# A two-layer diffusion trunk in float32 pairs: a reordered prologue, factors that change engine, and a shorter inverse root

## The chip, the cores and the metric

The kernel runs on one core of one Trainium2 chip. The metric is the device time of one launch, in microseconds (us): the median of the runs shown. The core has five instruction queues that run side by side and are tied together by semaphores: PE (matrix product, with PEld for its weight loads), DVE (VectorE), ACT (ScalarE), POOL (GpSimd) and SP, which here issues every DMA. Each queue runs in the order in which it was written.

## The reference

There are 512 latent and 256 context tokens of width 1024, and two layers. Each layer normalises (root mean square), scales and shifts the stream with vectors that come from a conditioning vector c ("adaLN": `c @ w_ada + b_ada`, six vectors of 1024 a layer), and projects the result with one wide matrix `w_in`. Four mixers work on pieces of that projection:

```
a = s5_branch(...)      # diagonal complex state space, both directions, GLU
b = sgu_branch(...)     # u * (W_s @ layer_norm(v) + b), blocks of 128 tokens
c = ssd_branch(...)     # silu(conv3(xbc)), chunked scan, rms_norm(y * silu(z))
d = mla_branch(...)     # q, k = rms_norm(.) * g, rotary part, softmax(q k^T / sqrt(96)) v
out = sum_i sigmoid(gate_i) * (y_i @ w_branch[i]) @ w_out
```

A residual, a second normalisation and a SwiGLU feed-forward follow. The output is the latent stream after layer two; context reads only context.

## The kernel before

Activations are kept transposed: a tile holds 128 channels on its partitions and the tokens along its rows (context 0 to 255, latents 256 to 767). A float32 product is made of three products of rounded halves (`mm3`): each weight tile is cast on ACT (`whi`), the remainder is made on POOL or DVE (`wlo`), and each activation likewise has a high and a low part (`hh`, `hl`; tiles `h`, `g` or `f`). PE accumulates in two PSUM banks `acc` and, for all else, in four banks `b`. A bank is free for the next product only when the last engine that reads it is done.

**Order.** The program is written once, as Python generators that interleave the mixers (`mix`), and a scheduler then fixes each engine's order with its own timing model; the trace shows how that order runs on the chip. In `mix`, the attention units (`attend`, two heads and 256 queries each) are interleaved with the gating unit (`sgu`), the state-space sixths (`s5_prep`, `s5_sixth`) and a filler made of wide projections at low priority: the convolution's input (`conv` in `mix`) and z. All of these share DVE. SP keeps eight loads in flight: the issue of a load waits until the load eight places ahead of it has landed.

**Prologue.** `run` loads the constants and c, then all six row blocks of the stream (`load_x`: context first), ten small parameter rows (`params_load`), eight column chunks of w_ada with 256 columns each (`ada_load`: rows of 1 KB), and the first 256 columns of w_in. `turn_x` transposes the stream on PE, `ada_chunk` multiplies a chunk and puts its result column-wise into `mod`, and `norm_mod` sums squares, takes `rsqrt` on DVE, spreads the result over partitions with a product against `ones`, and makes `hh` and `hl`.

**Places the change touches.** `rsqrt` (eleven short DVE instructions) is called by every normalisation: norm_mod, the attention's q and k, sgu and ssd. `mla_pair` scales each head with its token's factor and the learned gain by one `stt` a head, six a tile; `attend_unit` divides the exponentials by their sums on DVE; `conv`'s callback reads its PSUM bank five times (DVE, DVE, DVE, then ACT writes the tanh back into the bank, then DVE):

```
s.ts(a, ps, w(1), q["cb"][:, c:c + 1], ALU.mult, ALU.add)
... two stt that read ps shifted by a token ...
s.act(ps, a, AF.Tanh)
s.stt(a, ps, 1.0, a, ALU.add, ALU.mult)
```

In `ssd` the carried-in part of a chunk's output enters a PSUM bank as a 128-wide product with the identity, and the chunk's own part is added by products that are 64 wide, two to a bank column.

## Time and profile before

| | before |
|---|---|
| median of 3 runs | 2835.06 us (2834.6 to 2836.26) |
| profiled execution: span from first to last instruction | 2833.9 us (no other time of that execution is listed; 1.2 us below the median) |
| PE busy | 2639.4 us, 93% |
| DVE busy | 1562.5 us, 55%, 3402 instructions |
| ACT busy | 870.4 us, 31%, 1693 instructions |
| POOL busy | 1210.8 us, 43% |
| mean granted TensorE clock | 0.974 |

A busy share is a mean over stages with different limits. Three kinds of view are read below: the sum of a stretch (windows), the order of time (timeline), and the idle time of an engine by what ended it (waits). In waits and timelines the part behind `<-` names the engine and tile that came last.

### The profile page before, as it was taken

How to read it: one execution, taken by the hardware profiler on the slowest of the kernel's cores; microseconds unless marked ns; L12 is line 12 of the kernel's file. 1: busy time of each engine (PE TensorE's matmuls, PEld its weight loads, DVE VectorE, ACT ScalarE, POOL GpSimd, SP SyncE). 2: the span in 40 equal slices, each digit the busy share in tenths (PEclk: the TensorE clock that was granted, in tenths of full speed). 3: DMA queues.
4: the chain of work that ended last, by engine and by line, in shares of the span. 5: the costliest groups of instructions: out<-in, count | busy, mean ns of one | idle time of the engine just before them, and what ended most of it. 6: DMA issues, size and time to landing. Idle time of an engine off the chain costs nothing. (4 is left out here: it accounts for less than half of the span.)

```text
span 2833.9 us, 40144 instructions
## 1 busy us (share of the span) xinstructions
PE 2639.4 (93%) x14950; PEld 2147.7 (76%) x14950; DVE 1562.5 (55%) x3402; ACT 870.4 (31%) x1693; POOL 1210.8 (43%) x901
## 2 busy tenths in 40 slices
PE   6998898999999987999999999899999989899999
PEld 4777676777888875888888877777666866678887
DVE  6678989758453769543221245677836546422111
ACT  4233332342232333222212234333343223322222
POOL 2254444314432836554333334442423537344543
PEclk9999899999999998999999999999999989999999
DMA  7655454454444645323322335556445536323332
GB/s 247 175 176 188 138 168 141 145 162 143 138 155 149 213 139 169 108 91 94 97 76 60 94 98 159 179 175 192 139 152 167 167 127 206 114 84 105 104 97 82
DMA packets 430106, 397.46 MB, mean 140 GB/s; under 512 B 52292, under 2 KB 379640, under 8 KB 429816
## 3 DMA queue, kind: packets, MB, share of 16 engines
q1 hardware_dynamic: 429912, 394.91, 45.4%
q8 instruction: 118, 1.93, 0.3%
q14 instruction: 76, 0.62, 0.1%
HBM read 305.79 MB, written 89.05 MB: 139 GB/s over the span
## 5 line engine op out<-in xcount | busy, mean ns | idle before, releaser
L174 POOL TENSOR_TENSOR wlo<-raw,whi 128x1024 fp32r<-128x1024 f32 (+2 forms) x314 | 632.3, 2015 | 1064.9 <-ACT whi L169 982.9
L193 PE MATMUL acc<-h,whi 128*128 128x512 f32 (+2 forms) x3424 | 1020.8, 368 | 30.6 <-DVE gs L186 22.6
L193 PE MATMUL acc<-h,wlo 128*128 128x512 f32 (+1 forms) x2024 | 745.8, 369 | 7.8 <-DVE wlo L174 5.1
L193 PEld LDWEIGHTS acc<-h,whi 128*128 128x128 f32 (+1 forms) x3424 | 612.0, 191 | 142.4 <-DVE gs L186 25.7
L169 ACT CAST whi<-raw 128x1024 fp32r<-128x1024 f32 (+2 forms) x390 | 324.9, 834 | 817.1 <-PE b L193 304.8
L193 PEld LDWEIGHTS acc<-h,wlo 128*128 128x128 f32 x2024 | 384.5, 190 | 76.4 <-DVE wlo L174 7.1
L193 PE MATMUL acc<-g,whi 128*128 128x512 f32 (+1 forms) x840 | 271.4, 396 | 20.4 <-DVE g L174 8.5
L193 PE MATMUL acc<-f,whi 128*128 128x512 f32 (+1 forms) x600 | 230.2, 393 | 6.3 <-POOL f L174 5.2
L193 PE MATMUL b<-g,whi 128*128 128x256 f32 (+1 forms) x840 | 215.7, 335 | 3.3 <-ACT whi L169 3.3
L193 PE MATMUL b<-h,wlo 128*128 128x256 f32 (+1 forms) x624 | 203.6, 326 | 2.1 <-POOL wlo L174 2.1
L193 PE MATMUL b<-h,whi 128*128 128x256 f32 (+1 forms) x624 | 203.4, 326 | 0.0
L193 PEld LDWEIGHTS acc<-g,whi 128*128 128x128 f32 x840 | 153.9, 193 | 56.4 <-DVE g L174 11.9
L193 PE MATMUL b<-f,whi 128*128 128x256 f32 (+1 forms) x600 | 186.7, 321 | 1.7 <-ACT whi L169 1.7
L193 PE MATMUL b<-g,g 128*64 128x128 f32 (+5 forms) x915 | 180.4, 357 | 8.0 <-ACT g L171 5.2
L193 PEld LDWEIGHTS b<-g,whi 128*128 128x128 f32 x840 | 148.8, 193 | 28.4 <-ACT whi L169 6.5
L193 PE MATMUL acc<-g,wlo 128*128 128x512 f32 (+1 forms) x372 | 148.2, 398 | 4.7 <-DVE wlo L174 4.5
L186 DVE SCALAR_TENSOR_TENSOR sc<-sc,acc 128x512 f32<-128x512 f32 (+1 forms) x45 | 30.6, 680 | 219.6 <-ACT sc L171 219.6
L193 PEld LDWEIGHTS b<-g,g 128*128 128x128 f32 (+2 forms) x915 | 121.1, 182 | 34.2 <-issue 13.5
L174 POOL TENSOR_TENSOR g<-sc,g 128x256 fp32r<-128x256 f32 (+2 forms) x81 | 88.2, 1090 | 126.7 <-ACT g L169 87.9
L193 PEld LDWEIGHTS acc<-f,whi 128*128 128x128 f32 x600 | 112.8, 189 | 31.5 <-POOL f L174 6.7
L174 POOL TENSOR_TENSOR f<-f,f 128x384 f32<-128x384 f32 (+2 forms) x84 | 102.8, 1229 | 78.7 <-DVE f L174 35.0
L174 POOL TENSOR_TENSOR g<-g,sc 128x512 f32<-128x512 f32 (+1 forms) x82 | 103.0, 1268 | 75.8 <-DVE g L186 37.9
(257 smaller groups left out, 4013.2 us busy)
## 6 DMA issues: line engine op xcount, KB each, us to landing
raw<-in_w_in_dram SPq DMA_DIRECT2D x50, 1024.0 KB
raw<-in_w_ffn_in_dram SPq DMA_DIRECT2D x88, 512.0 KB
raw<-in_w_ada_dram SPq DMA_DIRECT2D x41, 1024.0 KB
raw<-in_w_ffn_out_dram SPq DMA_DIRECT2D x36, 512.0 KB
gate<-gs SPq DMA_DIRECT2D x32, 384.0 KB
f<-s5w SPq DMA_DIRECT2D x48, 256.0 KB
raw<-in_w_branch_dram SPq DMA_DIRECT2D x32, 384.0 KB
gs<-gate SPq DMA_DIRECT2D x32, 384.0 KB
```

The costliest lines, as they stand in the source:

```text
L169: s.nc.scalar.copy(out=out, in_=x)
L174: (e or s.nc.vector).tensor_tensor(out=out, in0=a, in1=b, op=op)
L186: s.nc.vector.scalar_tensor_tensor(out=out, in0=a, scalar=sc, in1=b, op0=op0, op1=op1)
L193: s.nc.tensor.matmul(out=out, lhsT=l, rhs=r, start=start, stop=stop)
```

## The change

Six edits. (1) The prologue loads three parameter rows and the four latent blocks, then four w_ada chunks of 512 columns (rows of 2 KB), then the two context blocks, then the other small rows; latents are transposed first, context last. (2) `rsqrt` has nine instructions in place of eleven. (3) In `mla_pair` one product with a broadcast replaces six `stt` a tile; the gain goes into the evacuation of the transposes (a per-partition factor on ACT and DVE) and into rotary tables made once a layer on DVE (`rot`), with four more small loads a layer into `gain`. (4) These scalings move from DVE to ACT: the softmax division, the value rows of `mla_pair`, the first step of `conv`, and sgu's normalisation (with one small DVE instruction more). (5) `conv` writes its tanh to an SBUF tile instead of its PSUM bank. (6) The identity product in `ssd` is made in two halves of 64 columns.

```diff
@@ -200,16 +200,18 @@
-        shape = list(x.shape)
-        hx, t = s.ty(shape), s.ty(shape)
+        t, u = s.ty(list(x.shape)), s.ty(list(x.shape))
         s.ts(y.bitcast(I32), x.bitcast(I32), -0.5, float(0x5F3759DF), ALU.mult, ALU.add)
-        s.ts(hx, x, -0.5)
-        for _ in range(3):
-            s.mul(t, y, y)
-            s.mul(t, t, hx)
-            s.stt(y, t, 1.5, y, ALU.add, ALU.mult)
+        s.mul(t, y, y)
+        s.mul(t, t, x)
+        s.ts(u, t, 0.375, -1.25, ALU.mult, ALU.add)
+        s.mul(u, u, t)
+        s.stt(y, u, 1.875, y, ALU.add, ALU.mult)
+        s.stt(t, y, -0.5, y, ALU.mult, ALU.mult)
+        s.mul(t, t, x)
+        s.stt(y, t, 1.5, y, ALU.add, ALU.mult)
@@ -295,12 +297,13 @@
-        return s.params_rest(l, s.params_load(l))
-    def params_load(s, l):
+        return s.params_rest(l, s.params_load(l)[0])
+    def params_load(s, l, first=10):
...
+        later = []
@@ -311,10 +314,12 @@
-            s.dma.dma_start(out=rows[at:at + n, :], in_=ap)
+            later.append((rows[at:at + n, :], ap))
...
-        return rows, names, at
+        for o, ap in later[:first]:
+            s.dma.dma_start(out=o, in_=ap)
+        return (rows, names, at), lambda: [s.dma.dma_start(out=o, in_=ap) for o, ap in later[first:]]
@@ -336,7 +341,18 @@
-        q["qn"], q["kn"] = bc("qn", t["mla_q_norm"][l], 96), bc("kn", t["mla_k_norm"][l], 96)
+        q["rot"] = {}
+        gain = q["gain"] = s.keep("gain", [96, 4])
+        s.nc.vector.memset(gain, 1.0)
+        for i, (part, ap) in enumerate((("q", t["mla_q_norm"][l]), ("kv", t["mla_k_norm"][l]))):
+            g = bc("gn" + part, ap[64:96], 32).rearrange("p (o a d) -> p o a d", o=1, a=2).to_broadcast([P, 4, 2, 16])
+            gt = q["rot"][part] = s.keep("rot" + part, [P, 2, 4, 2, 16])
+            for j, c in enumerate((K_COS, K_SIN)):
+                cs = s.k[:, c:c + 64].rearrange("p (b o d) -> p b o d", b=4, o=1).to_broadcast([P, 4, 2, 16])
+                s.mul(gt[:, j], g, cs)
+            s.dma.dma_start(out=gain[:, 2 * i:2 * i + 1], in_=ap.rearrange("(d o) -> d o", o=1))
+            s.dma.dma_start(out=gain[:64, 2 * i + 1:2 * i + 2], in_=ap[:64].rearrange("(d o) -> d o", o=1))
@@ -369,47 +385,47 @@
-    def ada_load(s, l, i, tag="raw"):
-        src = s.t["w_ada"][l][:, 256 * i:256 * i + 256].rearrange("(k p) f -> p k f", p=P)
-        out = []
-        pool, step = {"raw": (s.rp, KD), "h": (s.hp, 3), "f": (s.fp, 2)}[tag]
-        for k in range(0, KD, step):
-            n = min(step, KD - k)
-            raw = pool.tile([P, n, 256], F32, tag=tag, name=s.nm(tag))
-            s.dma.dma_start(out=raw, in_=src[:, k:k + n])
-            out += [raw[:, j] for j in range(n)]
+    def ada_load(s, l, i, tags=("raw",), w=256):
+        src = s.t["w_ada"][l][:, 256 * i:256 * i + w].rearrange("(k p) f -> p k f", p=P)
+        out, each = [], KD // len(tags)
+        for h, tag in enumerate(tags):
+            pool, size = {"raw": (s.rp, 2048), "h": (s.hp, 768), "f": (s.fp, 512)}[tag]
+            n = min(each, size // w)
+            for k in range(each * h, each * h + each, n):
+                raw = pool.tile([P, n, w], F32, tag=tag, name=s.nm(tag))
+                s.dma.dma_start(out=raw, in_=src[:, k:k + n])
+                out += [raw[:, j] for j in range(n)]
         return out
-    def ada_chunk(s, a, i, raw=None):
+    def ada_chunk(s, a, i, raw=None, w=256):
         raw = s.ada_load(a["l"], i) if raw is None else raw
-        both = s.acc() if a["l"] == 0 or i >= 8 else s.b1()
-        ps = both[:, :256]
+        nb = w // P
+        ps = (s.acc() if a["l"] == 0 or i >= 8 else s.b1())
+        p2 = (ps[:, 256:] if nb == 2 else s.b1()).rearrange("p (b j v) -> p b j v", b=nb, j=4)
+        ps = ps[:, :w]
...
-        s.act(part[:, :256], ps)
-        p2 = both[:, 256:].rearrange("p (b j v) -> p b j v", b=2, j=4)
-        for b in range(2):
+        s.act(part[:, :w], ps)
+        for b in range(nb):
             s.tr(p2[:, b], part[:, b * P:(b + 1) * P])
-        m = a["m"]
-        s.nc.vector.tensor_reduce(out=m[:, 2 * i:2 * i + 2, :], in_=p2[:, :, :, 0:2].rearrange("p b j v -> p b v j"),
-                                  axis=AX.X, op=ALU.add)
-        s.add(m[:, 2 * i:2 * i + 2, :], m[:, 2 * i:2 * i + 2, :],
-              a["q"]["b_ada"][:, 2 * i:2 * i + 2].unsqueeze(2).to_broadcast([P, 2, 2]))
-        j, c = i // 4, slice(2 * (i % 4), 2 * (i % 4) + 2)
-        m = m[:, 2 * i:2 * i + 2, :]
+        m = a["m"][:, 2 * i:2 * i + nb, :]
+        s.nc.vector.tensor_reduce(out=m, in_=p2[:, :, :, 0:2].rearrange("p b j v -> p b v j"), axis=AX.X, op=ALU.add)
+        s.add(m, m, a["q"]["b_ada"][:, 2 * i:2 * i + nb].unsqueeze(2).to_broadcast([P, nb, 2]))
+        j, c = i // 4, slice(2 * (i % 4), 2 * (i % 4) + nb)
...
-            s.stt(v, m, 1.0, g.unsqueeze(2).to_broadcast([P, 2, 2]), ALU.add, ALU.mult)
+            s.stt(v, m, 1.0, g.unsqueeze(2).to_broadcast([P, nb, 2]), ALU.add, ALU.mult)
@@ -420,18 +436,17 @@
+        raw = s.rp.tile([P, 2, D], F32, tag="raw", name=s.nm("raw"))
         for b in range(NB):
-            if b == 4:
-                raw = s.rp.tile([P, 2, D], F32, tag="raw", name=s.nm("raw"))
-            x = raw[:, b - 4] if b >= 4 else s.wp.tile([P, D], F32, tag="whi" if b % 2 else "wlo", name=s.nm("xr"))
-            src = s.t["ctx"][0, b * P:(b + 1) * P, :] if b < 2 else s.t["x"][0, (b - 2) * P:(b - 1) * P, :]
-            s.dma.dma_start(out=x, in_=src)
-            out.append(x)
-        return out
+            out.append(raw[:, b] if b < 2 else s.wp.tile([P, D], F32, tag="whi" if b % 2 else "wlo", name=s.nm("xr")))
+        src = lambda b: s.t["ctx"][0, b * P:(b + 1) * P, :] if b < 2 else s.t["x"][0, (b - 2) * P:(b - 1) * P, :]
+        for b in range(2, NB):
+            s.dma.dma_start(out=out[b], in_=src(b))
+        return out, lambda: [s.dma.dma_start(out=out[b], in_=src(b)) for b in range(2)]
...
-        for b in range(0, NB, 2):
+        for b in (2, 4, 0):
@@ -550,8 +565,9 @@
+            s.stt(x, mv[:, :, 0], -1.0, r, ALU.mult, ALU.mult)
             for j in range(2):
-                s.ts(vn[:, j, :], vn[:, j, :], mv[:, j, 0:1], r[:, j:j + 1], ALU.subtract, ALU.mult)
+                s.act(vn[:, j, :], vn[:, j, :], AF.Identity, scale=r[:, j:j + 1], bias=x[:, j:j + 1])
@@ -629,7 +645,7 @@
-                    s.ts(vt[:, b, hs, :], pv[:, :, 64:P], r[:, b:b + 1])
+                    s.act(vt[:, b, hs, :], pv[:, :, 64:P], AF.Copy, scale=r[:, b:b + 1])
@@ -646,20 +662,16 @@
-        gn = q["qn"] if part == "q" else q["kn"]
+        gt, gc = q["rot"][part], q["gain"][:, 2 * (part == "kv") + (off == CTX):][:, :1]
...
-            for h in range(6):
-                s.stt(x[:, h, :w], x[:, h, :w], rr[:, b, h:h + 1], gn[:, :w], ALU.mult, ALU.mult)
+            s.mul(x[:, :, :w], x[:, :, :w], rr[:, b, :].unsqueeze(2).to_broadcast([P, 6, w]))
             if part == "kv":
-                kg = s.ty([P, 1, 32])
-                s.mul(kg, kr[:, b:b + 1, :], gn[:, 64:].unsqueeze(1))
-                s.mul(x[:, :, 64:96], kg.to_broadcast([P, 6, 32]), rs[:, b, :].unsqueeze(2).to_broadcast([P, 6, 32]))
+                s.mul(x[:, :, 64:96], kr[:, b:b + 1, :].to_broadcast([P, 6, 32]), rs[:, b, :].unsqueeze(2).to_broadcast([P, 6, 32]))
             if off == CTX:
-                cs, sn = (s.k[:, j + 16 * (b0 + b):j + 16 * (b0 + b) + 16].unsqueeze(1).unsqueeze(1).to_broadcast([P, 6, 2, 16])
-                          for j in (K_COS, K_SIN))
+                cs, sn = (gt[:, i, b0 + b].unsqueeze(1).to_broadcast([P, 6, 2, 16]) for i in range(2))
@@ -670,8 +682,8 @@
-            s.act(y[:, 0:3], ps[0][:96])
-            s.vcopy(y[:, 3:6], ps[1][:96])
+            s.act(y[:, 0:3], ps[0][:96], AF.Copy, scale=gc)
+            s.ts(y[:, 3:6], ps[1][:96], gc)
@@ -724,7 +736,7 @@
-                s.ts(p[b][:, :nk * P], p[b][:, :nk * P], ri[:, b:b + 1])
+                s.act(p[b][:, :nk * P], p[b][:, :nk * P], AF.Copy, scale=ri[:, b:b + 1])
@@ -856,7 +868,8 @@
-                    s.mm(o, yoff[:, 2 * c:2 * c + 2, :].rearrange("p h e -> p (h e)"), s.ident, stop=False)
+                    for h2 in range(2):
+                        s.mm(o[64 * h2:64 * h2 + 64, :], yoff[:, 2 * c + h2, :], s.ident, stop=False)
@@ -1333,11 +1346,12 @@
-                s.ts(a, ps, w(1), q["cb"][:, c:c + 1], ALU.mult, ALU.add)
+                s.act(a, ps, AF.Identity, scale=w(1), bias=q["cb"][:, c:c + 1])
...
-                s.act(ps, a, AF.Tanh)
-                s.stt(a, ps, 1.0, a, ALU.add, ALU.mult)
+                z = s.sc()[:, :n]
+                s.act(z, a, AF.Tanh)
+                s.stt(a, z, 1.0, a, ALU.add, ALU.mult)
@@ -1490,17 +1504,19 @@
-        xr = s.load_x()
-        rows = s.params_load(0)
-        order = (0, 4, 1, 5, 2, 6, 3, 7)
-        aw = [s.ada_load(0, i, tag) for i, tag in zip(order, ["raw"] + 5 * ["h"] + 2 * ["f"])]
+        rows, more = s.params_load(0, 3)
+        xr, x_ctx = s.load_x()
+        order = (0, 4, 2, 6)
+        aw = [s.ada_load(0, i, tags, 512) for i, tags in zip(order, (("h", "h"), ("h", "h"), ("f", "f"), ("f", "raw")))]
+        x_ctx()
+        more()
...
-            s.ada_chunk(a, i, w)
+            s.ada_chunk(a, i, w, 512)
```

Three places of the new order matter for what follows; in the rows a name is tile, number, `<-` and what it reads.

In the prologue SP's queue reaches the first w_in load (`raw_197` before, `raw_207` now) so; before:

```order
L379 DMA f_195<-in_w_ada_dram 128x2x256
L479 DMA raw_197<-in_w_in_dram 128x8x256
L334 DMA alog_313<-in_ssd_a_log_dram 128x12
L334 DMA dtb_315<-in_ssd_dt_bias_dram 128x12
L334 DMA qn_317<-in_mla_q_norm_dram 128x96
```

Now, the last eleven rows of the small loads ahead of it:

```order
L339 DMA gnq_329<-in_mla_q_norm_dram 128x32
L354 DMA gain_327<-in_mla_q_norm_dram 96x1
L355 DMA gain_327<-in_mla_q_norm_dram 64x1
L339 DMA gnkv_336<-in_mla_k_norm_dram 128x32
L354 DMA gain_327<-in_mla_k_norm_dram 96x1
L355 DMA gain_327<-in_mla_k_norm_dram 64x1
L360 DMA bs_343<-in_sgu_b_s_dram 64x3x128
L361 DMA dd_344<-in_ssd_d_dram 64x3x1
L360 DMA bs_343<-in_sgu_b_s_dram 64x3x128
L361 DMA dd_344<-in_ssd_d_dram 64x3x1
L494 DMA raw_207<-in_w_in_dram 128x8x256
```

The load stood directly behind w_ada; now nineteen small loads and the context (which shares its tile's buffer) stand between. On DVE, in the same stretch, the context's copies (`g_213`, `g_215`, ...) now stand behind the rotary tables:

```order
L174 TENSOR_TENSOR sc_452<-sc_452,sc_472 128x512
L174 TENSOR_TENSOR rotq_331<-gnq_329,k 128x128 x2
L174 TENSOR_TENSOR rotkv_338<-gnkv_336,k 128x128
L458 COPY g_213<-b_285 128x256
L174 TENSOR_TENSOR rotkv_338<-gnkv_336,k 128x128
L458 COPY g_215<-b_293 128x256
L458 COPY g_217<-b_301 128x256
L458 COPY g_219<-b_309 128x256
L190 TENSOR_SCALAR hc_321<-prm_319 128x20
L416 TENSOR_REDUCE mod_349<-b_355 128x8
```

So these copies, and what stands behind them, follow the small load `gnkv`.

Second place: POOL ahead of the first projection (h: low part of a normalised tile; wlo: remainder of w_in). Before:

```order
L174 TENSOR_TENSOR h_472<-sc_532,h_464 128x512
L174 TENSOR_TENSOR h_474<-sc_544,h_466 128x512
L174 TENSOR_TENSOR h_475<-sc_550,h_467 128x512
L174 TENSOR_TENSOR h_476<-sc_556,h_468 128x512
L174 TENSOR_TENSOR h_478<-sc_568,h_470 128x512
L174 TENSOR_TENSOR wlo_200<-raw_197,whi_199 128x1024
L174 TENSOR_TENSOR wlo_1101<-raw_197,whi_1100 128x1024
L174 TENSOR_TENSOR h_479<-sc_574,h_471 128x512
```

Now:

```order
L174 TENSOR_TENSOR wlo_210<-raw_207,whi_209 128x1024
L174 TENSOR_TENSOR wlo_1069<-raw_207,whi_1068 128x1024
L174 TENSOR_TENSOR h_444<-sc_502,h_436 128x512
L174 TENSOR_TENSOR h_446<-sc_514,h_438 128x512
L174 TENSOR_TENSOR h_447<-sc_520,h_439 128x512
L174 TENSOR_TENSOR h_448<-sc_526,h_440 128x512
L174 TENSOR_TENSOR h_450<-sc_538,h_442 128x512
L174 TENSOR_TENSOR h_451<-sc_544,h_443 128x512
```

The two remainders moved from behind five of the six low parts to ahead of all six.

Third place: DVE at the first convolution tile of layer one's mixing (`gs` is the result, `acc` its PSUM bank, `ty` and `g` the softmax sums and exponentials). Before:

```order
L190 TENSOR_SCALAR gs_4404<-acc_4405,hc_311 128x512
L174 TENSOR_TENSOR ty_4308<-ty_4308,ty_4312 128x2
L186 SCALAR_TENSOR_TENSOR gs_4404<-acc_4405,hc_311,gs_4404 128x511
L725 RECIPROCAL ty_4309<-ty_4308 128x2
L708 TENSOR_REDUCE ty_4334<-b_4331 128x2
L186 SCALAR_TENSOR_TENSOR gs_4404<-acc_4405,hc_311,gs_4404 128x511
L190 TENSOR_SCALAR g_4321<-g_4321,ty_4309 128x768
L190 TENSOR_SCALAR g_4322<-g_4322,ty_4309 128x768
L714 TENSOR_REDUCE ty_4338<-b_4340 128x1
L714 TENSOR_REDUCE ty_4338<-b_4343 128x1
L186 SCALAR_TENSOR_TENSOR gs_4404<-acc_4405,gs_4404 128x512
```

Now DVE has, and ACT has in its own queue:

```order
L174 TENSOR_TENSOR ty_4207<-ty_4207,ty_4211 128x2
L737 RECIPROCAL ty_4208<-ty_4207 128x2
L174 TENSOR_TENSOR f_5046<-f_5046,f_5047 128x512
L186 SCALAR_TENSOR_TENSOR gs_4275<-acc_4276,hc_321,gs_4275 128x511 x2
L186 SCALAR_TENSOR_TENSOR gs_4275<-sc_4304,gs_4275 128x512
```

```order
L171 ACTIVATE g_4221,ty_4211<-b_4215,ty_4206 128x512
L171 ACTIVATE gs_4275<-acc_4276,hc_321 128x512
L171 ACTIVATE g_4220<-g_4220,ty_4208 128x768
L171 ACTIVATE g_4221<-g_4221,ty_4208 128x768
L171 ACTIVATE sc_4304<-gs_4275 128x512
L169 CAST whi_4618<-raw_4616 128x1024
```

DVE's last read of the bank is now the second `stt`; the first step, the two divisions and the tanh stand in ACT's queue, the weight cast behind them.

## Rows read from the trace of the kernel before

**Rows 1.** The page, head and part 1: span, then busy time by engine.

```profile
span 2833.9 us, 40144 instructions
...
PE 2639.4 (93%) x14950; PEld 2147.7 (76%) x14950; DVE 1562.5 (55%) x3402; ACT 870.4 (31%) x1693; POOL 1210.8 (43%) x901
```

**Rows 2.** Windows of both mixing stages: busy PE, PEld, DVE, ACT, POOL; clock; DMA.

```profile
150.00:700.00 550.00, 490.33 (x3128) 397.21 (x3126) 442.77 (x1062) 193.51 (x464) 223.94 (x201) 0.95 0.50 156
...
1800.00:2320.00 520.00, 488.01 (x2802) 374.17 (x2801) 341.87 (x872) 176.67 (x386) 196.10 (x158) 0.97 0.52 161
```

**Rows 3.** Timeline of SP, 0 to 60 us: start, duration of issue, load.

```profile
14.94 0.40 SPq L379 DMA_DIRECT2D raw<-in_w_ada_dram  x1
...
37.41 0.37 SPq L479 DMA_DIRECT2D raw<-in_w_in_dram  x1
...
40.24 0.44 SPq L334 DMA_DIRECT2D qn<-in_mla_q_norm_dram  x1
...
46.05 0.60 SPq L345 DMA_DIRECT2D dd<-in_ssd_d_dram  x1
```

**Rows 4.** DMA, 0 to 60 us: rate in 40 slices of 1.5 us.

```profile
GB/s 0 217 154 363 401 418 421 370 54 4 40 328 369 350 352 348 347 348 348 352 346 348 348 346 348 350 349 347 331 174 56 0 15 186 389 398 410 422 408 432
```

**Rows 5.** Timeline of the prologue: start, duration, what, [idle before it].

```profile
20.36 1.93 PE L193 MATMUL acc<-raw,cT 128*32 128x256 f32 x16 [3.35 <-DMA raw<-in_w_ada_dram]
...
46.30 1.98 ACT L169 CAST whi<-raw 128x1024 fp32r<-128x1024 f32 x2
...
47.70 5.08 POOL L174 TENSOR_TENSOR wlo<-raw,whi 128x1024 fp32r<-128x1024 f32 x2
...
50.31 0.80 PE L193 MATMUL acc<-h,wlo 128*128 128x512 f32 x1 [0.76 <-POOL wlo L174]
...
62.77 0.59 PE L193 MATMUL b<-sc,ones 128*128 128x256 f32 x2
...
65.59 0.50 PE L193 MATMUL acc<-h,whi 128*128 128x256 f32 x2 [2.22 <-POOL h L174]
```

**Rows 6.** Waits of PE, 150 to 700 us: total us, times, longest.

```profile
PE acc L193 <- DVE gs L186: 14.1, 5, 5.1
PE b L197 <- DVE g L186: 11.7, 1, 11.7
PE b L193 <- DVE sc L443: 9.9, 5, 3.5
```

**Rows 7.** The same, 1700 to 2400 us.

```profile
PE acc L193 <- DVE gs L186: 8.5, 4, 3.5
```

**Rows 8.** Timeline at one convolution tile, 396 to 403 us.

```profile
399.04 0.74 DVE L186 SCALAR_TENSOR_TENSOR gs<-acc,hc,gs 128x511 f32<-128x511 f32 x1
...
401.94 0.68 DVE L186 SCALAR_TENSOR_TENSOR gs<-acc,gs 128x512 f32<-128x512 f32 x1
...
402.68 1.22 PE L193 MATMUL acc<-h,whi 128*128 128x512 f32 x2 [3.41 <-DVE gs L186]
```

**Rows 9.** Groups of DVE by form: count | busy us, mean ns | idle before.

```profile
L190 DVE TENSOR_SCALAR g<-g,ty 128x768 f32<-128x768 f32 x48 | 31.2, 690 | 0.3
...
L186 DVE SCALAR_TENSOR_TENSOR g<-g,ty,kn 128x64 f32<-128x64 f32 x72 | 21.7, 365 | 0.0
...
L174 DVE TENSOR_TENSOR ty<-ty 128x2 f32<-128x2 f32 x68 | 19.6, 289 | 1.4
...
L174 DVE TENSOR_TENSOR sc<-f,ty 128x384 f32<-128x384 f32 x20 | 14.5, 747 | 0.3
```

**Rows 10.** Groups of ACT by form, the same columns.

```profile
L171 ACT ACTIVATE g<-b,ty 128x256 f32<-128x256 f32 x60 | 28.3, 473 | 70.2 <-DVE ty L190 64.3 <-DVE ty L174 3.3 <-DVE ty L186 1.7
...
L169 ACT CAST g<-st 128x768 fp32r<-128x768 f32 x5 | 4.2, 836 | 9.0 <-DMA st<-mq 8.9
```

**Rows 11.** Groups of PE by form: the identity product, and half-width products.

```profile
L193 PE MATMUL b<-g,g 128*64 128x128 f32 x240 | 22.5, 303 | 0.0
...
L193 PE MATMUL b<-k,sc 128*128 128x128 f32 x60 | 14.8, 331 | 1.4 <-POOL sc L174 1.4
```

## Prediction

> **What bounds the kernel now.** I read the page first: PE is busy for 93% of a span of 2833.9 us [rows 1], so a gain is a stretch in which PE stands still or runs slowly. The sums by stretch then show where that is. In the mixing stage of layer one (150 to 700 us) PE is busy 490.3 of 550 us at a clock of 0.95, and DVE 442.8; in that of layer two (1800 to 2320 us) PE is busy 488.0 of 520 us at 0.97, and DVE 341.9 [rows 2]. That is 59.7 + 32.0 = 91.7 us of idle PE beside an engine that is 81% and 66% busy. The waits name it: of the first stage's idle time 14.1 us end with DVE's work on a convolution tile, 11.7 us (one wait) with DVE's scaling of an attention tile, and 9.9 us with DVE's copies of transposed probabilities [rows 6]; in the second the convolution takes 8.5 us [rows 7]. So here the bound is DVE's queue. The third place is the prologue: PE's projection runs steadily only from 50.31 us [rows 5].
>
> **The prologue, +8 us.** Before: one chunk of w_ada (1.05 MB) is issued at 14.94 us [rows 3] onto an empty queue and multiplied at 20.36 us [rows 5]: 5.4 us, of which 3.0 are data at 348 GB/s, so 2.4 are fixed. Rows of 4 KB (the stream, 4.5 to 12 us) move at 363 to 421 GB/s, rows of 1 KB (w_ada) at 346 to 352 [rows 4]. For rows of 2 KB there is no row; between 16 engines at 47 ns a piece (348) and 158 ns (415), a straight line gives 84 ns, 390 GB/s, my estimate; the ends are 348 and 415.
> Now: the latents' 2.1 MB are issued three small loads later (0.44 us each [rows 3]) and flow from about 5 to 10.3 us; w_ada's 8.39 MB take 21.5 us at 390, to 31.8; the context 2.5 us, to 34.3. In the old queue data ended near 44.3 us [rows 4] and the load waiting for it was issued at 46.05 [rows 3]: 1.7 us to completion, so 36.0 now. With eight loads in flight, the first broadcast load waits for that; `gnkv` is five issues behind it (0.46 us each, 38.3) and lands 2.4 us later, 40.7. DVE's queue holds the context's copies behind the tables made from it; two tables, three copies and the last transposes take about 1.9 us: 42.6. Only then is the context's buffer free for w_in, whose issue also stands behind ten more small loads, near 42 us. It lands 5.4 us later, at 48.1; before, it was there by 46.05. ACT casts it (1.98 us for two [rows 5]), POOL makes the two remainders (5.08 us for two [rows 5]) from 49.1 to 54.2, and only behind them the first low part of the activations (half as wide as a remainder, 1.27 us): PE starts at 55.5, not 50.31, +5.2. The 48 products take 12.4 us as before (50.31 to 62.77). The context's sum of squares then stands on PE behind the last of them, where before its spreading product was ready at 62.77, 2.8 us ahead of the context's first product [rows 5]; another inverse root, about 2.6 us, now lies between. Together +8. Bounds: +12 with w_ada at 348; -3 if none of the small loads is waited for and the hole at 12 to 15 us [rows 4] closes.
>
> **The convolution, -17 us.** In the tile shown the second `stt` ends at 399.8 us, but the bank is free only after the last one, at 402.6, because ACT's tanh and two softmax divisions lie between; PE stood for 3.4 us [rows 8]. Now nothing reads the bank after the second `stt`: 2.8 us earlier. The nine waits sum to 14.1 + 8.5 = 22.6 us [rows 6, 7], the longest 5.1; taking 2.8 us from each, or all of the shorter ones, leaves about 5. What may come late next is ACT, which now makes the first step. Bounds -23 and +5.
>
> **The softmax division, -5 us.** 48 divisions of 690 ns [rows 9] leave DVE, two in front of most of the copies that PE waited 9.9 us for [rows 6]: 1.4 us from each of five waits is 7, of which I take 5. On ACT one costs what a cast of the same size costs, 836 ns [rows 10], and ACT is busy only 193.5 and 176.7 us in the stages [rows 2]. Bounds -10, +5.
>
> **The rest of DVE's relief, -8 us.** Off DVE go 31.2 us of divisions, 21.7 us of 64-wide scalings [rows 9], 60 wider ones (at least 365 ns each, 22), some 65 instructions of conv, values, sgu and short divisions (near 0.5 us, estimated, 33), and 44 inverse roots by two instructions of 289 ns [rows 9], 25. On come ten products of 576 and twelve of 384 elements, at 747 ns for 384 [rows 9], 20 us. Net 113 of 785 us in the two stages, 14%. Of the 91.7 us of idle PE, 59 are neither convolution nor copies: 14% is 8. Bounds 0 and -20. A product of two tensors costs 1.95 ns an element and a division 0.90 [rows 9]. The Trainium skill (VectorE: DVE Perf Modes, "Why `tensor_tensor` can't do 2×_2P or 4×") speaks against this exchange: a float32 tensor with a scalar uses both read ports for one tensor and does two elements a cycle, two tensors cannot. With the new products at the division's price, the relief would be 11 us larger, and the sum 1 us lower; the trace agrees with the rule.
>
> **Inverse roots in the norms, -3 us.** Seven norms stand on PE's path, two instructions of 289 ns less each [rows 9], some shorter in a quiet queue: 3. Bounds 0, -6.
>
> **The identity product, -3 us.** Its 60 instructions are busy 14.8 us, 247 ns each; half-width ones 94 ns each [rows 11], so 120 make 11.3. Bounds -4 and, with the old busy time each, +15. The Trainium skill (TensorEngine Tiling (Array Packing), "Key Properties") says that a change of tiling mode drains the engine; here a full-width product stood between half-width ones, so by the rule the gain is more than the rows' 3.5 us. No row prices a drain.
>
> **The clock, -11 us.** At 0.95 of 490.3 us and 0.97 of 488.0 us [rows 2], 24.5 + 14.6 = 39 us of work are lost to the lower of the two levels (1.2 and 2.4 GHz). The three terms above remove 30 of 91.7 us of idle time, a third; I take 11. Bounds 0, -39.
>
> **New waits on ACT, +6 us.** In each of 30 softmax halves ACT's scaling waits for DVE's reciprocal, with evacuations and weight casts behind it. Waits of this kind exist: ACT waited 64.3 us for DVE's maxima [rows 10]. I take 0.2 us of PE a half; bounds 0 and +45 (1.5 us). The parameter loads of layer two and the tables lie beside the feed-forward and cost nothing there.
>
> Sum: 8 - 17 - 5 - 8 - 3 - 3 - 11 + 6 = -33. From the span of 2833.9 that is 2800.9; the median of the runs lies 1.2 us above the span, so 2802 us.
>
> **Rivals.**
> *More relief.* DVE's queue loosens as a whole, half of the 91.7 us goes, and the clock regains 20: -46 - 20 + 8 - 3 + 1 = -60, 2774 us. For it: DVE is named in all four large waits. Against: part of the idle time ends with other data.
> *Little relief.* The new order forms new waits in the same stages: convolution -12, norms -2, halves -3, clock -5, prologue +8, ACT +6: -8, 2827 us. For it: the order comes from a timing model, and each engine is bound to it. With the prologue at its upper bound, +12, this is 2831, no change.
> *Slower: ACT's queue.* Place: the softmax halves, where ACT now waits for DVE, and behind it the evacuations that free PE's banks. At 1.5 us of PE a half, 30 halves give +45 in place of +6, with all else as forecast: 2841 us. It decides from 1.3 us a half on, where 39 us eat up the other terms' 39. For it: 64.3 us of such waits [rows 10]. Against: ACT is 35% busy in these stages [rows 2].
>
> **How the numbers follow.** Forecast (2788 to 2822) 0.45, more relief 0.17, little relief 0.13, no change 0.08, slower 0.17. The range is 2772 to 2842: it holds most of the first four and about half of the slower case. A change within 0.2% (5.7 us) can't be told from none; faster is 0.45 + 0.17 + 0.13 = 0.75, same 0.08, slower 0.17.
>
> **What would show it.** Right: PE's first steady product near 55 us and the context's near 73; waits of PE for `gs` in the mixing stages near 5 us instead of 22.6; DVE's busy time near 1450 us (1562 less 113), ACT's near 935 (870, 40 for the 48 divisions and some 25 for the rest); a clock near 0.98. Wrong: w_in cast before 46 us (prologue); waits of PE for ACT's copies or casts that grow by more than 20 us (ACT's queue); the same idle time behind other names (little relief).

## The result and the profile after

The changed kernel takes 2803.2 us in the median of 4 runs (2799.7 to 2808.2), the kernel before 2834.8 (2829.4 to 2836.3): a ratio of 0.9899, 95% interval 0.9882 to 0.9916, or 28.6 us less (24 to 33); the medians lie 31.6 us apart. The prediction was 2802, 33 us less than before, in a range of 2772 to 2842. The total was right within a few microseconds; several of its terms were not, and they cancelled.

The page of the changed kernel, head and part 1, answers to [rows 1]:

```profile
span 2798.5 us, 39916 instructions
...
PE 2634.6 (94%) x14946; PEld 2139.2 (76%) x14946; DVE 1465.7 (52%) x3084; ACT 942.2 (34%) x1802; POOL 1211.7 (43%) x901
```

PE's work is 4.8 us shorter and its idle time falls from 194.5 to 163.9 us, 30.6 less: the gain is nearly all idle time, where the forecast had 11 of its 33 us as work at a higher clock. The two traced executions lie 35 us apart, some 7 more than the ratio says, so the last digits of what is read from them belong to them alone. DVE lost 97 us (113 forecast), ACT gained 72 (65 forecast). The windows of the two mixing stages, as in [rows 2], and the waits of PE in the first and in the second of them, as in [rows 6, 7]:

```profile
150.00:700.00 550.00, 509.42 (x3242) 408.17 (x3241) 401.19 (x917) 240.36 (x541) 236.81 (x208) 0.96 0.52 162
...
1800.00:2320.00 520.00, 493.46 (x2842) 376.96 (x2841) 318.97 (x735) 213.22 (x440) 214.38 (x173) 0.98 0.56 173
```

```profile
PE b L197 <- DVE g L174: 11.1, 3, 9.1
...
PE acc L193 <- DVE gs L186: 5.9, 6, 2.4
...
PE b L193 <- DVE sc L458: 2.1, 1, 2.1
...
PE acc L193 <- DVE gs L186: 3.3, 3, 1.6
```

The convolution's waits fall from 22.6 to 9.2 us, those for the copied probabilities from 9.9 to 2.1; the single long wait for an attention tile stays (11.7, now 9.1). PE's waits for ACT in these two stages, counted in layer two from the context's norm on, are 6.3 us together, 7.4 before; only in layer one's feed-forward do those for casts of weights grow, from 4.7 to 6.5.

The prologue, from PE's, ACT's, POOL's, DVE's and SP's timelines, as in [rows 3, 5]:

```profile
39.95 0.49 DVE L174 TENSOR_TENSOR rotq<-gnq,k 128x128 f32<-128x128 f32 x2 [19.09 <-DMA gnq<-in_mla_q_norm_dram]
...
42.28 1.54 PE L197 MATMUL b<-k,raw 128*128 128x128 f32 x6 [4.75 <-DVE g L458]
...
42.94 0.55 SPq L494 DMA_DIRECT2D raw<-in_w_in_dram  x1
...
50.84 1.99 ACT L169 CAST whi<-raw 128x1024 fp32r<-128x1024 f32 x2 [4.47 <-DMA raw<-in_w_in_dram]
...
51.96 4.92 POOL L174 TENSOR_TENSOR wlo<-raw,whi 128x1024 fp32r<-128x1024 f32 x2 [27.79 <-ACT whi L169]
...
58.34 1.22 PE L193 MATMUL acc<-h,whi 128*128 128x512 f32 x2 [4.98 <-POOL h L174]
...
72.06 0.60 PE L193 MATMUL b<-ones,sc 128*128 128x128 f32 x4
...
78.14 0.80 PE L193 MATMUL acc<-h,whi 128*128 128x256 f32 x2 [2.17 <-POOL h L174]
```

PE's steady products start 8.0 us later than before (58.34 against 50.31) and those of the context 12.5 us later; 5.2 and about 8 were forecast. How the distance to the kernel before grows and shrinks is read from starts of the same products in the timelines of PE (us against before, so a minus is earlier; the first column of numbers is before's own start; "spread" is the product with `ones` that spreads a norm's result):

| product | before | after | a_oldpro | a_tabpool | b_conv | b_convz | b_mla | b_div | b_half | b_rsqrt |
|---|---|---|---|---|---|---|---|---|---|---|
| context norm, spread | 62.8 | +12.5 | -1.6 | +12.1 | -1.1 | +1.5 | -0.6 | +0.2 | +0.9 | -1.0 |
| gating weights' sums, layer 1 | 367.9 | -5.3 | -20.5 | -8.3 | -2.4 | +4.4 | -22.9 | +1.0 | +0.2 | +3.8 |
| `ssda` sums, layer 1 | 657.4 | -4.8 | -21.3 | +5.7 | -8.8 | +13.0 | -4.8 | -9.7 | +6.1 | -2.6 |
| last group norm, layer 1 | 862.0 | -11.9 | -28.3 | -0.8 | -14.4 | +10.6 | -10.4 | -8.0 | -3.4 | +10.7 |
| context norm, layer 2 | 1722.8 | -13.4 | -26.6 | -0.8 | -13.8 | +6.7 | -8.7 | -9.7 | -2.2 | +3.1 |
| last group norm, layer 2 | 2310.1 | -35.1 | -46.5 | -21.8 | -20.2 | -0.2 | -13.8 | -13.3 | -11.3 | +2.4 |
| end of the last product | 2830.1 | -35.6 | -44.5 | -23.1 | -17.6 | -1.4 | -15.0 | -13.0 | -10.9 | +1.1 |

After: 12.5 us lost in the prologue, 24.4 regained in layer one's mixing, 1.5 in its feed-forward, 21.7 in layer two's mixing. (The later columns are the experiments.)

### The profile page after: what moved, and what is told of

Its sections match the earlier page's. It is cut to its first block, busy times and chain, and to the rows that moved or that the text cites. A ratio compares the mean times of both kernels' runs of the same rounds, so it can differ in the third digit from the quotient of the medians.

```text
span 2798.5 us, 39916 instructions
## 1 busy us (share of the span) xinstructions
PE 2634.6 (94%) x14946; PEld 2139.2 (76%) x14946; DVE 1465.7 (52%) x3084; ACT 942.2 (34%) x1802; POOL 1211.7 (43%) x901
## 5 line engine op out<-in xcount | busy, mean ns | idle before, releaser
L193 PE MATMUL acc<-h,whi 128*128 128x512 f32 (+2 forms) x3424 | 1024.6, 369 | 23.1 <-DVE gs L186 9.2
L193 PEld LDWEIGHTS acc<-g,whi 128*128 128x128 f32 x840 | 154.0, 193 | 54.6 <-DVE g L174 12.5
L186 DVE SCALAR_TENSOR_TENSOR sc<-sc,acc 128x512 f32<-128x512 f32 (+1 forms) x45 | 30.6, 681 | 219.9 <-ACT sc L171 219.9
```

Of the source, the lines that this page charges most:

```text
L186: s.nc.vector.scalar_tensor_tensor(out=out, in0=a, scalar=sc, in1=b, op0=op0, op1=op1)
L193: s.nc.tensor.matmul(out=out, lhsT=l, rhs=r, start=start, stop=stop)
```

## The experiments

Each kernel was timed beside the kernel before; times are medians of 4 to 12 executions and ratios are to that kernel, with 95% intervals. 0.001 is 2.8 us. `...` in code marks lines left out. "Waits in the two stages" are those from 150 to 700 and from 1700 to 2400 us.

### a_oldpro: the changed kernel with the old prologue

```
-        rows, more = s.params_load(0, 3)
-        xr, x_ctx = s.load_x()
-        order = (0, 4, 2, 6)            # four chunks of 512
...
+        xr = s.load_x()                 # context first
+        rows = s.params_load(0)[0]
+        order = (0, 4, 1, 5, 2, 6, 3, 7)  # eight chunks of 256
...
```

> The changed kernel with the prologue of before (context first among the blocks, eight chunks of 256 columns, all parameter loads ahead of them); every other edit stays. In the changed kernel PE's first steady product came at 58.34 us instead of 50.31 and the context's first product at 78.14 instead of 65.59. Theory (the prologue's loss is paid at the end): the first steady product is back near 50 us and the time is 8 to 12.5 us below the changed kernel's 2803, so 2791 to 2795. Rival (slack in the mixing stage takes the delay up): 2801 to 2805. Rival (the tables made from gnkv cost as much here, since they stand in DVE's queue in the old order too): first steady product at 54 us or later and 2797 or more.

2791.5 us, 0.9857 (0.9836 to 0.9878): 11.9 us under the changed kernel by the ratios (4 to 20). The first theory stands: the prologue's loss is paid at the end. It is the fastest of the kernels measured (o_evac below is its equal). What it shows of the order, on PE:

```profile
24.54 1.16 PE L193 MATMUL b<-ones,sc 128*128 128x128 f32 x8
...
29.75 1.13 PE L193 MATMUL b<-sc,ones 128*128 128x512 f32 x2 [1.11 <-DVE sc L190]
...
48.61 0.79 PE L193 MATMUL acc<-h,wlo 128*128 128x512 f32 x1 [0.61 <-POOL wlo L174]
```

The latents' sum of squares and its inverse root stand between the chunks, at 24.5 to 30 us. In the changed kernel they stand behind the last one, at 47.2 and 51.3.

### a_tabpool, a_winfirst, a_both: what sets the prologue's start

Tables on POOL; w_in issued ahead of the small loads, with the context in a buffer of its own; both.

```
-                s.mul(gt[:, j], g, cs)
+                s.mul(gt[:, j], g, cs, s.nc.gpsimd)      # a_tabpool, a_both
...
-        raw = s.rp.tile([P, 2, D], F32, tag="raw", ...)   # context's rows
+        half = lambda: s.g([P, 512])                      # a_winfirst, a_both
...
-        more()
         ws = s.weights(s.t["w_in"][0], C_CQ, BR)
         first = next(ws)
+        more()                                            # a_winfirst, a_both
```

> The changed kernel with the four rotation tables made by POOL instead of DVE, nothing else. Theory (the issue of w_in behind twelve small loads on SP's queue sets the start, the tables stand beside it): PE's context transposes go on near 37.5 us instead of 42.28, but w_in still lands near 50 us, so the first steady product comes at 57 to 58 us and the time is 2801 to 2804. Rival (the tables in DVE's queue set the start): first steady product 4 to 5 us earlier, near 53.5 us, and 2797 to 2799.

> The changed kernel with the context's rows in four tiles of another pool, so that w_in's first load needs no buffer of theirs, and that load issued ahead of the small parameter loads; tables on DVE as in the changed kernel. Theory (w_in's place in SP's queue and the tables in DVE's queue each set a chain of nearly the same length): w_in lands by 39 us, the two remainders are done by 45 us, and the start is then set by the tables and what follows them: 56 to 57 us, time 2801 to 2803. Rival (w_in's landing alone sets the start): first steady product at 51 to 53 us, time 2796 to 2798.

> The two edits of the two kernels before this one together: w_in issued ahead of the small loads, tables on POOL. Theory (two chains of nearly the same length): only now does the start move, to 51 to 53 us, and the time is 5 to 7 us below the changed kernel's, 2796 to 2798. Rival (one of the two alone sets the start): the same time as the better one of the two. Rival (the parameter rows, which now land behind w_in, set the start): 56 us or later, 2801 or more.

a_tabpool: 2814.1 us, 0.9928 (0.9911 to 0.9945), slower than expected by any theory. a_winfirst: 2801.9, 0.9893 (0.9877 to 0.9909), as the first theory said. a_both: 2806.8, 0.9921 (0.9900 to 0.9941); its first theory fell, and the numbers of its third (56 us or later, 2801 or more) came true. The prologues of a_tabpool (PE), a_winfirst (ACT, PE) and a_both (POOL, DVE, PE):

```profile
45.37 1.67 PE L193 MATMUL b<-sc,ones 128*128 128x512 f32 x2 [3.39 <-DVE sc L190]
...
58.62 1.22 PE L193 MATMUL acc<-h,whi 128*128 128x512 f32 x2 [11.57 <-POOL h L174]
```

```profile
39.24 1.99 ACT L169 CAST whi<-raw 128x1024 fp32r<-128x1024 f32 x2 [1.20 <-DMA raw<-in_w_in_dram]
...
56.50 1.22 PE L193 MATMUL acc<-h,whi 128*128 128x512 f32 x2 [2.98 <-POOL h L174]
```

```profile
45.39 4.64 POOL L174 TENSOR_TENSOR wlo<-raw,whi 128x1024 fp32r<-128x1024 f32 x2
...
45.37 0.16 DVE L190 TENSOR_SCALAR ty<-b 128x4 f32<-128x4 f32 x1 [0.83 <-PE b L193]
45.57 2.19 DVE L190 TENSOR_SCALAR ty<-ty 128x4 int32<-128x4 int32 x1
47.79 2.26 DVE L174 TENSOR_TENSOR ty<-ty 128x4 f32<-128x4 f32 x1
50.09 0.16 DVE L174 TENSOR_TENSOR ty<-ty,ty 128x4 f32<-128x4 f32 x1
...
39.70 0.28 PE L197 MATMUL b<-k,sc 98*128 98x98 f32 x1 [2.19 <-DMA sc<-in_ssd_conv_w_dram]
...
52.40 2.07 PE L193 MATMUL b<-sc,ones 128*128 128x512 f32 x2 [7.06 <-DVE sc L190]
...
57.44 1.22 PE L193 MATMUL acc<-h,whi 128*128 128x512 f32 x2 [2.97 <-POOL h L174]
```

Two chains meet at the start. With the norm 6 us early (a_tabpool) PE still waits to 58.6 for POOL, which makes w_in's remainders; with w_in cast at 39 (a_winfirst) it waits to 56.5 for the norm. With both, the norm's inverse root falls into POOL's two remainders: two of its instructions on 512 numbers take 2.19 and 2.26 us instead of 0.17, each as long as one remainder, and the start is 57.4. These two stops are 4.1 us of it. Of the third theory's cause, the parameter rows behind w_in, the trace shows 2.2 us, PE's wait at 39.70; no run separates the two.

The other news is a_tabpool's total: its start is the changed kernel's, yet it is 8 us slower by the ratios (1 to 15) and ends 12.5 us later in the traces, all of it lost in layer one's mixing (-8.3, then +5.7 in the table). PE's waits for `gs` there are 13.6 us instead of 5.9. The longest, on POOL, DVE and PE:

```profile
403.81 0.68 DVE L174 TENSOR_TENSOR f<-ty,f 128x512 f32<-128x512 f32 x1
...
407.95 2.34 POOL L174 TENSOR_TENSOR wlo<-raw,whi 128x1024 fp32r<-128x1024 f32 x1
...
408.06 2.78 DVE L174 TENSOR_TENSOR f<-ty,f 128x512 f32<-128x512 f32 x1
410.77 0.73 DVE L186 SCALAR_TENSOR_TENSOR gs<-acc,hc,gs 128x511 f32<-128x511 f32 x1
...
411.65 1.20 PE L193 MATMUL acc<-h,whi 128*128 128x512 f32 x2 [6.54 <-DVE gs L186]
```

PE waits 6.5 us for the bank's last reader, which stands in DVE's queue behind a product that takes 2.78 us beside POOL's remainder (0.68 for the same form at 403.81 us). From 238 us on DVE's instructions come in another order than in the changed kernel: moving four small products out of the prologue has laid the queues out anew, 200 us away from them.

### b_conv, b_convz: the convolution alone

The kernel before with both edits (b_conv), and with the tanh's tile alone (b_convz):

```
-                s.ts(a, ps, w(1), q["cb"][:, c:c + 1], ALU.mult, ALU.add)
+                s.act(a, ps, AF.Identity, scale=w(1), bias=q["cb"][:, c:c + 1])   # b_conv only
...
-                s.act(ps, a, AF.Tanh)
-                s.stt(a, ps, 1.0, a, ALU.add, ALU.mult)
+                z = s.sc()[:, :n]
+                s.act(z, a, AF.Tanh)
+                s.stt(a, z, 1.0, a, ALU.add, ALU.mult)
```

> The kernel before with the convolution's two edits alone (ACT makes the first step, the tanh goes to a tile in SBUF). Theory of the prediction (the bank is released 2.8 us earlier): PE's waits for gs in the two mixing stages fall from 22.6 us to about 5, and the time is 15 to 20 us below the before of the same chip, near 2816. Rival (PE waits for the place of the second step in DVE's queue, which this edit leaves alone): gs waits of 12 us or more in all, time 0 to 8 us below before, 2824 to 2832.

> The kernel before with only the convolution's tanh written to a tile in SBUF; its first step stays on DVE. Theory of the prediction (the early release of the bank is what counts): nearly all of the gain of both edits together, which was 16 us, so 12 to 18 us below before; PE's waits for gs in the two mixing stages at 15 us or less. Rival (what counts is the 28 first steps that leave DVE's queue and move the rest of it): 0 to 5 us below before, gs waits near 20 us.

b_conv: 2817.6 us, 0.9943 (0.9926 to 0.9960), 16 us less: the size that was forecast, but with waits of 15.3 us, not 5. b_convz: 2835.2, 1.0000 (0.9989 to 1.0011): nothing. PE's waits for `gs` in the two stages, of b_conv (with those for copied probabilities in the first) and of b_convz:

```profile
PE acc L193 <- DVE gs L186: 9.6, 5, 3.5
PE b L193 <- DVE sc L443: 1.6, 2, 1.0
...
PE acc L193 <- DVE gs L186: 5.7, 3, 3.5
```

```profile
PE acc L193 <- DVE gs L186: 10.8, 6, 4.8
...
PE acc L193 <- DVE gs L186: 8.2, 3, 3.7
```

Of b_conv's 16 us only 7.3 are waits for `gs`; another 8.3 are the waits for copied probabilities (9.9 to 1.6 in the first stage), which the edit does not touch. Releasing the bank early buys 3.6 us of waits and no time. What differs is the first steps that left DVE, 19 in the trace before (the expectation says 28), 12.8 us of its work. Whether the 16 us come from that shorter queue or from the new order that the scheduler made with it, no run separates.

### b_mla, b_div: the attention's edits alone

b_mla is the kernel before with the projections' new code (`mla_pair`, tables, gains, value rows scaled by ACT; its main lines first), b_div with the division on ACT:

```
-            for h in range(6):
-                s.stt(x[:, h, :w], x[:, h, :w], rr[:, b, h:h + 1], gn[:, :w], ALU.mult, ALU.mult)
+            s.mul(x[:, :, :w], x[:, :, :w], rr[:, b, :].unsqueeze(2).to_broadcast([P, 6, w]))
...
```

```
-                s.ts(p[b][:, :nk * P], p[b][:, :nk * P], ri[:, b:b + 1])
+                s.act(p[b][:, :nk * P], p[b][:, :nk * P], AF.Copy, scale=ri[:, b:b + 1])
```

> The kernel before with the attention projections' edits alone (one broadcast product in place of six scalings, gains in the rotation tables and in the evacuations, values scaled by ACT). Theory of the prediction (relief of DVE by its share, 22 + 22 us less, 20 us more): 3 to 5 us below before, 2827 to 2829. Theory from the two traces (the stage of the attention projections, 75 to 303 us, became 11.6 us shorter between kernel before and changed kernel): 8 to 12 us below before, 2820 to 2824. In the old prologue's order the tables should cost nothing: first steady product at 50 us.

> The kernel before with the softmax division alone on ACT. Theory of the prediction: PE's waits for DVE's copies of transposed probabilities fall from 9.9 to about 4 us, and the time is 3 to 7 us below before, near 2827. Rival (ACT's queue): waits of PE for ACT's copies and casts grow by more than 10 us and the time is at or above before, 2832 to 2842. Rival (a looser DVE queue is worth more than the waits that name it): 2815 to 2822.

b_mla: 2819.3 us, 0.9948 (0.9931 to 0.9966), 15 us less, more than either of its theories; b_div: 2825.9, 0.9966 (0.9954 to 0.9977), 10 less, between its first theory and its last. b_mla's waits for `gs`, with the convolution untouched:

```profile
PE acc L193 <- DVE gs L186: 2.2, 2, 1.2
...
PE acc L193 <- DVE gs L186: 1.0, 2, 0.7
```

They are 3.2 us, less than the convolution's own edit leaves (15.3). So PE's wait hangs on what else stands in DVE's queue; the tile it is booked on is the one that comes last. b_mla had gained 22.9 us by the gating weights and gave 18 back before `ssda`, in the same stage. b_div's PE waits for ACT, counted as above, are 3.4 and 4.9 us (3.1 and 4.3 before): no queue on ACT.

### b_half, b_rsqrt: the two small edits

```
-                    s.mm(o, yoff[:, 2 * c:2 * c + 2, :].rearrange("p h e -> p (h e)"), s.ident, stop=False)
+                    for h2 in range(2):
+                        s.mm(o[64 * h2:64 * h2 + 64, :], yoff[:, 2 * c + h2, :], s.ident, stop=False)
```

> The kernel before with only the identity product in two halves. Theory of the prediction: the form's busy time falls from 14.8 to near 11 us and the time by 3, to within 1 to 5 us below before. It takes no work from any engine but PE, so what it changes beyond that is the order in which the engines' queues are laid out. Rival (order): the time goes 8 us or more to either side, and the difference lies outside the stretches in which the product stands.

> The kernel before with only the shorter inverse root (9 instead of 11 DVE instructions). Theory of the prediction: 3 us in the seven norms on PE's path and about 2 us as its part of DVE's relief, so 4 to 6 us below before. Rival (only the norms): 1 to 3 us. Rival (order): 8 us or more to either side.

(b_rsqrt takes over the nine-instruction `rsqrt` of the change's diff.) b_half: 2828.7 us, 0.9976 (0.9962 to 0.9989), 7 less where 1 to 5 were expected. b_rsqrt: 2842.3, 1.0028 (1.0016 to 1.0040), 8 more. b_half's forms, against [rows 11]:

```profile
L193 PE MATMUL b<-g,g 128*64 128x128 f32 x240 | 19.8, 276 | 0.0
...
L193 PE MATMUL b<-k,sc 128*64 128x128 f32 x120 | 12.2, 281 | 1.4 <-POOL sc L174 1.4
```

The halves take 12.2 us instead of 14.8, and their unchanged neighbours 19.8 instead of 22.5: 5.3 us together. In the six traced kernels with the full-width product the neighbours take 21.1 to 22.9 us, in the eight with the halves 19.4 to 19.8. The traces agree here with the Trainium skill (TensorEngine Tiling (Array Packing), "Key Properties"), by which a change of tiling mode drains TensorE, as a full-width product between half-width ones would bring it; the drain alone is not priced by them. b_rsqrt's DVE has 27 us less to do [rows 1], and PE's waits for `gs` rise from 22.6 to 28.1 us:

```profile
PE 2645.9 (93%) x14950; PEld 2151.0 (76%) x14950; DVE 1535.5 (54%) x3314; ACT 872.3 (31%) x1693; POOL 1204.1 (42%) x901
...
PE acc L193 <- DVE gs L186: 18.7, 6, 8.4
...
PE acc L193 <- DVE gs L186: 9.4, 3, 4.8
```

That is what the rival of order expected. It is a loss alone; why the new layout is worse stays open. Beside the other single edits it shows that work taken off DVE does not give the gain: 12 us less of it go with 16 us of time in b_conv, 40 with 10 in b_div, 43 with 15 in b_mla, and 27 with a loss of 8 here.

### o_evac, o_wide: a better version

The fast kernel a_oldpro with a copy of the convolution's bank to SBUF by ACT (o_evac), and with the wide chunks in the old order (o_wide):

```
+                u = s.sc()[:, :n]
+                s.act(u, ps)                 # the two stt then read u
```

```
+        order = (0, 4, 2, 6)                 # after load_x and params_load of before
+        aw = [s.ada_load(0, i, tags, 512) ...]
```

> The changed kernel with the prologue of before, and a second ACT pass over the convolution's bank, a plain copy to SBUF, so that DVE's two steps read no bank and PE waits for ACT alone. Theory (PE's wait stands for the second step's place in DVE's queue): the waits for gs by DVE, 5.9 + 3.3 us in the changed kernel's two stages, go, ACT's work grows by 20 copies of 0.57 us and 10 shorter ones, and the time is 3 to 8 us below the 2791.5 of the kernel without the copy, 2784 to 2788. Rival (ACT's longer queue and the fifth tile of the shared pool give it back): 2791 to 2796.

> The changed kernel with the load order of before (context first, all parameter loads ahead of the modulation's columns) and the chunks of 512 columns kept. Theory (2 KB rows moved at 383 to 403 GB/s in the changed kernel against 346 to 352 for 1 KB rows, so 8.39 MB take 2.6 us less, and nothing else in the prologue's chain gets longer): w_in lands 2 to 3 us earlier than with the narrow chunks, first steady product 45 to 47 us, time 2788 to 2790 against 2791.5. Rival (the wide chunk's sum stands longer on PE and its first product starts later, behind a longer load): 2792 to 2798.

o_evac: 2794.4 us, 0.9857 (0.9834 to 0.9880): the rival, no gain. PE's waits for `gs` fall from 7.4 us (a_oldpro) to 6.0, and 4.4 us of waits for the new copies come instead. o_wide: 2801.7, 0.9880 (0.9864 to 0.9897), 6.5 us slower than with narrow chunks by the ratios, with an interval of -1 to 14. Its prologue, on DVE and PE:

```profile
44.01 2.09 DVE L174 TENSOR_TENSOR mod<-mod,prm 128x8 f32<-128x8 f32 x1
46.13 2.26 DVE L186 SCALAR_TENSOR_TENSOR gs<-mod,prm 128x8 f32<-128x8 f32 x1
...
41.81 1.06 PE L193 MATMUL b<-ones,sc 128*128 128x128 f32 x8
51.66 2.04 PE L193 MATMUL b<-sc,ones 128*128 128x512 f32 x2 [8.79 <-DVE sc L190]
```

w_in is cast at 42.45 us instead of 44.74, 2.3 us earlier. But with four wide chunks the order puts the norm's sum behind the last one, at 41.8 us (24.5 with narrow ones), DVE's queue in front of the inverse root waits for the tables' loads and then for POOL, and the start is 56.7 us. In a_oldpro the steady products start at 48.6, in the changed kernel at 58.3: by these starts 8 of the 10 us of delay come with the wide chunks, which move the norm to the end of the chain; the totals alone are too close to show it. Both theories had looked at the load and PE's sums alone.

## Why the prediction was right, step by step

| step | forecast | measured alone |
|---|---|---|
| prologue | +8 (-3 to +12) | +12 (+4 to +20), after against a_oldpro |
| convolution | -17 (-23 to +5) | -16 (-21 to -11); release alone 0 (-3 to +3) |
| softmax division | -5 (-10 to +5) | -10 (-13 to -7) |
| attention projections, in "the rest of DVE's relief", -8 in all | some -4 | -15 (-20 to -10) |
| inverse roots | -3, and some -2 in the relief | +8 (+5 to +11) |
| identity product | -3 (-4 to +15) | -7 (-11 to -3) |

The six add to 12 - 16 - 10 - 15 + 8 - 7 = -28, give or take 12, against -28.6 for the whole change (errors taken as independent, between the two ratios of the prologue too). Each measured value has its own share of the clock in it, which the forecast kept apart. The gating's normalisation was not tried alone. With such intervals, and layouts that move by 8, so close a sum is partly luck. So is the prediction's total: the clock's and the inverse roots' gains, which did not come, and a dearer prologue were made good by a division and projections worth more than was thought and by waits on ACT that stayed away.

**The prologue.** The wait forecast for w_in holds: issued at 42.94 (42 forecast), cast at 50.84 (48.1), remainders from 51.96 (49.1). Two reasons given were wrong. The load lands 7.9 us after its issue, not 5.4, beside the activations' first stores; whether they slow it is not shown. And the latents' norm was taken for ready, since it was before: it ends only at 56.5 us by a_winfirst, so mending w_in alone is worth 1.8 us. The rest of the 12.5 us at the context: the forecast let the 48 products take 12.4 us, but four of them had run at 47.43 us, ahead of the row taken for the start; all 48 now take 13.7 (58.34 to 72.06). From there to the context's first product it is 6.1 us, 2.8 before (62.77 to 65.59). The estimate of 390 GB/s for 2 KB rows was good: the chunks' load reads 382 to 403 in the changed kernel (first 62 us, 40 slices).

```profile
GB/s 0 242 102 362 381 383 332 361 399 402 398 386 383 390 389 385 389 390 382 388 403 402 104 1 13 10 14 69 59 40 351 383 412 375 366 405 418 371 193 11
```

**The convolution.** The step "now nothing reads the bank after the second `stt`: 2.8 us earlier" failed: b_convz does that and gains nothing (-3 to +3 us). The 16 us came with the first step's move to ACT, half of them as shorter waits for another tile. The tile that the profile names as releaser was a symptom.

**DVE's relief.** The sum of work was close: the broadcast products cost 18.6 us against 20 (twelve of 384 elements 11.5, ten of 576 7.1); here two misses cancel, since the forecast's 1.95 ns an element is 2.6 for the first (997 ns each in the mean) and 1.3 for the second (754). Its worth was mis-sized: a share of 14% of the idle time was assumed, while the division and the projections alone bring 25 us. Nor does the gain of the single edits go with how much left DVE. PE's waits that end with DVE, over the whole run, are 128 us before and 106 after; 112 in b_conv, 117 in b_div, 103 in b_mla, 133 in b_rsqrt.

**The inverse roots** failed in sign, -5 against +8: DVE's work did shrink, by 27 us (25 forecast), but PE's waits grew (b_rsqrt). **The identity product** went as forecast, its busy time to 12.2 us (11.3), and its neighbours gained as much again.

**The clock** failed as a term: 0.974 before and after. In the two stages the time lost to the lower level falls from 39 to 30 us (20.4 + 9.9 by the windows above), 9 of the 11 forecast; the prologue takes it back. Windows of the first 150 us, before and after:

```profile
0.00:60.00 60.00, 38.90 (x244) 24.19 (x245) 35.53 (x90) 26.00 (x53) 16.39 (x23) 0.91 0.88 290
60.00:150.00 90.00, 85.17 (x496) 70.96 (x496) 61.70 (x254) 25.87 (x43) 27.99 (x18) 0.98 0.55 154
```

```profile
0.00:60.00 60.00, 37.18 (x144) 17.61 (x145) 20.83 (x61) 18.83 (x35) 11.23 (x19) 0.86 0.81 290
60.00:150.00 90.00, 84.36 (x458) 69.87 (x458) 67.74 (x271) 27.75 (x48) 26.32 (x18) 0.92 0.47 138
```

By the same sum that is 5 us before and 12 after: 7 of the 9.

**New waits on ACT**, +6, did not show, and the rival of ACT's queue is out. So are the other two by their times, 2774 and 2827. Each had a part of the truth. "More relief" let DVE's queue loosen as a whole, and waits did fall that an edit does not touch; but of the two stages' 91.7 us of idle PE 24.6 went, not half (the forecast had 30). "Little relief" had new orders with new waits in the same stages, and b_rsqrt and a_tabpool are such. ACT waits 16.3 us for the reciprocals of the divisions, but 42.5 instead of 64.3 for the maxima.

## What to carry to other kernels

A wait of the busiest engine names the instruction that came last, not what made it late: before shortening that instruction, ask what stands ahead of it in its queue, and change the queue there, then measure, since less work in it did not always help. Where a scheduler lays out the queues, a small edit can move the time by 8 us, here in a stage that it does not touch, so a gain below that is read from the stage's own waits and from single edits, not from one total. A wider load saves transfer time and can still lose, if the work that used to fit between the narrow ones then queues behind the last.

## What the runs showed that was not expected

Tiny DVE instructions can stop for as long as a POOL product runs: 2.19 and 2.26 us instead of 0.17 in a_both, 2.09 and 2.26 in o_wide, each beside one remainder of 2.3 to 2.4 us. A DVE product that reads PSUM beside the changed kernel's remainders (53.39 us) kept its 0.69 us. The Trainium skill (SBUF — State Buffer, "Who interferes with whom") names a cause, a port pair shared by the two engines and held for a whole instruction. The rows agree with it; no run here tests it against another. It cost some 4 us in the prologue of a_both and as much in that of o_wide.
